# Four modulation products on the four column groups of TensorE, in place of two and two

## The chip, the cores and the metric

One core of one Trainium2 chip runs the whole program in a single launch. The metric is the device time of that launch in microseconds (us); 1860.03 us is the median of the three runs before the change.

## The reference, cut to what matters

The reference computes one layer of a hybrid decoder for a prompt of 1024 tokens and for 8 samples of 8 tokens: gated linear attention beside latent attention, then a feed-forward block with a short convolution. Before all of it stands the modulation, computed from one vector per sequence:

```python
mod = jax.nn.silu(c) @ lw['w_ada'] + lw['b_ada']
sh1, sc1, gt1, sh2, sc2, gt2 = [m[:, None, :] for m in jnp.split(mod, 6, axis=-1)]
h = rmsnorm(x, lw['g_pre_mix']) * (1.0 + sc1) + sh1
z = h @ lw['w_in']
...
x = x + gt1 * rmsnorm(mix, lw['g_post_mix'])
h2 = rmsnorm(x, lw['g_pre_ffn']) * (1.0 + sc2) + sh2
...
x = x + gt2 * rmsnorm(y, lw['g_post_ffn'])
```

There are nine vectors `c` (one for the prompt, eight for the samples) of 1024 values, and `w_ada` is 1024 x 6144 in float32, so each of the six sections of `mod` is the product of a 9 x 1024 matrix with a 1024 x 1024 matrix.

## The kernel before, in words

The kernel is written in Python against a tile framework. The program is traced in program order; a planner then puts the instructions of each engine into an order by a simulation of its own, by priority (which follows program order) and by when it thinks that operands and buffers are ready. A tile taken from a pool waits until one of the pool's buffers of that tag is free; any free buffer serves.

**A section of the modulation** (`ada_section`, line 235) has two halves of 512 columns. For one half, the sum over 1024 rows is cut into eight parts of 128 rows (`k` = 0 to 7). The stationary operand is `cT[:, k]`, 128 x 32 (nine columns used), the moving one a piece of `w_ada` of 128 x 512. Part k goes to the group of 32 columns of TensorE with number k mod 4, so its result lands on partitions 32 (k mod 4) to 32 (k mod 4) + 31 of the tile `adaps`; parts k and k + 4 add up in the same place. A float32 product shows in the trace as two matmul instructions with two weight loads. The four partial sums are added later: by a small product with a selection matrix (`mod_T`, line 292, tile `modps`) for sections 0, 1, 3 and 4, and by VectorE (`ada_gate`, line 261, tiles `gpart` and `M`) for the gate sections 2 and 5. The weights come in tiles `wraw` of 128 x 2 x 512 (512 KB), one for two parts. So a half has four steps, each a load and two products (four matmul instructions on two column groups), and a `yield` behind each.

**Who drives it.** The program's first stage (`phase1`, line 352) runs sections 1 and 0 to their end at once (lines 382 and 388), with 16 buffers of `wraw`. The other four sections (3, 4, 2, 5) belong to the generator `ada` (line 437). It is advanced by one `next(ada, None)` ahead of each group of products of the input projection: nine times in the loop over the key and value columns (line 486, the tile `zps` has 320 columns there), twelve times in the loop over q and k (line 509, 384 or 320 columns), and nine times in each of the two loops over v and r (line 537, 512 columns). The first six of these 39 calls run `gates`; the next 32 are the modulation's steps; the last one finishes. A group of the projection is 24 matmuls (`mm3`, lines 141 to 143: high and low parts of float32 values).

**The buffers.** In this part `wraw` has four buffers, which the steps share with the projection's weights: `load_w` (line 280) loads a `wraw` tile, ScalarE copies it to `whi` (line 288), VectorE or GpSimd makes `wlo` (line 122), and then the buffer is free. `whi` and `wlo` have six buffers each, and a set of weights (`group`, line 398) takes four, so two of the next set's four loads keep their `wraw` buffers until the set in use is done with. All loads and nearly all stores are issued by SyncE (its queue is SP) in the planner's order.

Behind this stage follow the queries, gated linear attention interleaved with the attention over the samples' cached keys (to about 915 us), the output projection and the two halves of the feed-forward block.

Of the kernel before, what the change touches and what calls it, by code (L numbers as in the profile page):

```python
# [11 lines left out]
F32 = mybir.dt.float32  # L12
# [9 lines left out]
P = 128  # L22
D = 1024
# [83 lines left out]
class Kernel:  # L107
# [127 lines left out]
    def ada_section(self, sec, wp, pp, bufs, evac, rp=None):  # L235
        nc, A = self.nc, self.A
        w = A["w_ada"][0].rearrange("(a p) n -> p a n", p=P)
        rb = bufs[0]
        for half in range(2):
            ps = pp.tile([P, 512], F32, name="adaps", tag="A")  # L240
            for k2 in range(4):
                c0 = sec * D + half * 512
                raw = (rp or wp).tile([P, 2, 512], F32, name="wraw", tag="wraw", bufs=rb)
                nc.sync.dma_start(raw, w[:, 2 * k2:2 * k2 + 2, c0:c0 + 512])

                for kk in range(2):
                    k = 2 * k2 + kk
                    r = slice(32 * (k % 4), 32 * (k % 4) + 32)
                    nc.tensor.matmul(ps[r], self.cT[:, k, :], raw[:, kk, :], start=(k < 4), stop=(k > 3))
                yield 0.5  # L250
            evac(ps, half)

# [1526 lines left out]
```

## Time and profile before

| | |
|---|---|
| median of 3 runs (1857.51 to 1861.93) | 1860.03 us |
| the profiled execution's own time | 1861.26 us |
| its span, first to last instruction | 1859.5 us |
| TensorE busy in it | 1797.6 us (97%) |
| mean granted clock of TensorE | 0.985 of full speed |

The three runs lie within 0.24% of each other. The span is the stretch that the profile shows; the execution's own time is 1.76 us longer. The sums below are made against the profiled execution.

### The profile page before, as it was taken

How to read it: one execution, taken by the hardware profiler on the slowest of the kernel's cores; microseconds unless marked ns; L12 is line 12 of the kernel's file. 1: busy time of each engine (PE TensorE's matmuls, PEld its weight loads, DVE VectorE, ACT ScalarE, POOL GpSimd, SP SyncE). 2: the span in 40 equal slices, each digit the busy share in tenths (PEclk: the TensorE clock that was granted, in tenths of full speed). 3: DMA queues.
4: the chain of work that ended last, by engine and by line, in shares of the span. 5: the costliest groups of instructions: out<-in, count | busy, mean ns of one | idle time of the engine just before them, and what ended most of it. 6: DMA issues, size and time to landing. Idle time of an engine off the chain costs nothing.

```text
span 1859.5 us, 30758 instructions
## 1 busy us (share of the span) xinstructions
PE 1797.6 (97%) x12403; PEld 1500.4 (81%) x12403; DVE 930.1 (50%) x1680; ACT 708.9 (38%) x1398; POOL 529.8 (28%) x567
## 2 busy tenths in 40 slices
PE   6999999999999999999799999999999999999998
PEld 3888766765665776777499999999999999788787
DVE  3731233347784555565556755554545554523433
ACT  2461111455666666667523422222222222323322
POOL 2640100423554223323011133333333331202221
PEclk7999999999999999999899999999999999999999
DMA  8255552666655555455542412111222111834463
GB/s 300 87 160 181 181 172 75 248 210 199 212 197 166 203 196 173 161 184 181 181 149 104 137 65 71 65 59 65 72 70 70 65 61 61 266 98 136 146 183 96
DMA packets 170618, 265.26 MB, mean 143 GB/s; under 512 B 18278, under 2 KB 118694, under 8 KB 162283
## 3 DMA queue, kind: packets, MB, share of 16 engines
q1 hardware_dynamic: 156138, 179.39, 29.8%
q0 software_dynamic: 14336, 83.89, 13.0%
q8 instruction: 98, 1.61, 0.4%
q14 instruction: 46, 0.37, 0.1%
HBM read 221.49 MB, written 41.75 MB: 142 GB/s over the span
## 4 chain that ended last, share of the span: by engine, by line
PE 70%; DVE 3%; DMA 2%; ACT 1%; issue 1%; SPq 0%; POOL 0%; DVEq 0%; POOLq 0%; ACTq 0%
PE ups L141 9%; PE ups L143 9%; PE ups L142 9%; PE kps L1227 6%; PE yps L143 4%; PE yps L141 4%; PE yps L142 4%; PE S L1237 3%; PE O L1271 3%; PE y L141 2%; PE y L143 2%; PE y L142 2%; PE S L1239 1%; PE lps L705 1%; PE sps L141 1%; PE sps L142 1%
## 5 line engine op out<-in xcount | busy, mean ns | idle before, releaser
L141 PE MATMUL ups<-gh,uhi 128*128 128x384 f32 (+1 forms) x1056 | 347.2, 329 | 0.3 <-DVE hraw L343 0.3
L142 PE MATMUL ups<-gl,uhi 128*128 128x384 f32 (+1 forms) x1056 | 346.7, 328 | 0.0
L143 PE MATMUL ups<-gh,ulo 128*128 128x384 f32 (+1 forms) x1056 | 346.5, 328 | 0.0
L1565 DVE TENSOR_SCALAR cv<-u,vt 128x1024 f32<-128x1024 f32 (+1 forms) x88 | 133.2, 1535 | 216.3 <-ACT u L1555 179.3
L141 PEld LDWEIGHTS ups<-gh,uhi 128*128 128x128 f32 x1056 | 198.3, 188 | 0.7 <-DVE hraw L343 0.6
L143 PEld LDWEIGHTS ups<-gh,ulo 128*128 128x128 f32 x1056 | 198.3, 188 | 0.1
L142 PEld LDWEIGHTS ups<-gl,uhi 128*128 128x128 f32 x1056 | 198.3, 188 | 0.0
L1229 ACT COPY KT<-kps 128x512 f32<-128x512 f32 x256 | 145.3, 587 | 101.3 <-PE kps L1227 100.3
L122 POOL TENSOR_TENSOR ulo<-uraw,uhi 128x2048 fp32r<-128x2048 f32 x24 | 111.4, 4643 | 207.6 <-ACT uhi L1393 204.7
L1555 ACT COPY u<-ups 128x384 f32<-128x384 f32 (+1 forms) x130 | 57.6, 444 | 278.7 <-PE ups L143 278.7
L1227 PEld LDWEIGHTS kps<-ident,L 128*128 128x128 f32 x1024 | 111.5, 141 | 62.0 <-issue 43.4
L1227 PE MATMUL kps<-ident,L 128*128 128x128 f32 x1024 | 153.3, 280 | 4.1 <-ACT KT L1229 2.5
L143 PE MATMUL yps<-uhi,gl 128*128 128x512 f32 x341 | 133.3, 392 | 5.2 <-DVE gl L122 5.2
L141 PE MATMUL yps<-uhi,gh 128*128 128x512 f32 x341 | 133.2, 391 | 0.0
L142 PE MATMUL yps<-ulo,gh 128*128 128x512 f32 x341 | 133.1, 391 | 0.0
L122 DVE TENSOR_TENSOR gl<-graw,gh 128x1408 fp32r<-128x1408 f32 x31 | 59.1, 1908 | 130.2 <-ACT gh L1612 130.2
L1218 POOL DMA_INDIRECT R<-cache_krope,idx x64 | 66.5, 1039 | 179.3 <-PE kps L1227 141.4
L1612 ACT CAST gh<-graw 128x1408 fp32r<-128x1408 f32 (+1 forms) x35 | 45.7, 1306 | 158.7 <-PE yps L142 130.1
L1393 ACT CAST uhi<-uraw 128x2048 fp32r<-128x2048 f32 (+1 forms) x38 | 70.8, 1862 | 92.5 <-PE ups L142 67.1
L141 PE MATMUL zps<-whi,hh 128*128 128x512 f32 (+2 forms) x256 | 96.0, 375 | 0.0
L143 PE MATMUL zps<-whi,hl 128*128 128x512 f32 (+2 forms) x256 | 94.2, 368 | 0.8 <-DVE hl L122 0.8
L1571 POOL TENSOR_TENSOR gl<-gl,cv 128x1088 f32<-128x1088 f32 x22 | 56.0, 2544 | 135.3 <-ACT gl L1570 135.3
(443 smaller groups left out, 3803.5 us busy)
## 6 DMA issues: line engine op xcount, KB each, us to landing
wraw<-w_ada SPq DMA_DIRECT2D x48, 512.0 KB
uraw<-w_ffn_up SPq DMA_DIRECT2D x22, 1024.0 KB
graw<-s_g SPq DMA_DIRECT2D x32, 704.0 KB
s_g<-gl SPq DMA_DIRECT2D x22, 544.0 KB
uraw<-w_ffn_down SPq DMA_DIRECT2D x10, 1024.0 KB
xt<-x_prompt SPq DMA_DIRECT2D x16, 512.0 KB
wraw<-w_in SPq DMA_DIRECT2D x12, 512.0 KB
uraw<-w_o SPq DMA_DIRECT2D x4, 1024.0 KB
```

Source lines behind the costliest of these rows:

```text
L122: eng.tensor_tensor(out, x, hi.bitcast(F32), ALU.subtract)
L141: mm(out, wh, xh, start=start, stop=False)
L142: mm(out, wh, xl, start=False, stop=False)
L143: mm(out, wl, xh, start=False, stop=stop)
L1218: nc.gpsimd.indirect_dma_start(R.rearrange("p j l -> p (j l)"), None, ck, io)
L1227: nc.tensor.transpose(ps[:, k], x, self.ident)
L1229: nc.scalar.copy(KT[:, q // 2, j0:j0 + 4] if q < 4 else KR[:, 4 * half:4 * half + 4], ps)
L1237: nc.tensor.matmul(S[r], Q[:, c], KT[:, c, :, r], start=(c == 0), stop=False)
L1393: self.nc.scalar.copy(hi, raw)
L1555: copy(u[:, 2 + c0:2 + c0 + m], ps[:, 0:m])
L1565: nc.vector.tensor_scalar(yv[z], sh(2)[z], self.cw2[:, ch:ch + 1], self.cb[:, ch:ch + 1], ALU.mult, ALU.add)
L1571: nc.gpsimd.tensor_tensor(gl, gl, res[0], ALU.mult)
```

## The change

A half of a section takes two loads of `wraw` (four parts) in one step, yields, and in the next step runs the four products on the four column groups, one after the other in program order; then the same for the other four parts. The number of loads, of products and of yields stays. A step now is either two loads or four products (eight matmul instructions).

```diff
         for half in range(2):
             ps = pp.tile([P, 512], F32, name="adaps", tag="A")
-            for k2 in range(4):
-                c0 = sec * D + half * 512
-                raw = (rp or wp).tile([P, 2, 512], F32, name="wraw", tag="wraw", bufs=rb)
-                nc.sync.dma_start(raw, w[:, 2 * k2:2 * k2 + 2, c0:c0 + 512])
-
-                for kk in range(2):
-                    k = 2 * k2 + kk
-                    r = slice(32 * (k % 4), 32 * (k % 4) + 32)
-                    nc.tensor.matmul(ps[r], self.cT[:, k, :], raw[:, kk, :], start=(k < 4), stop=(k > 3))
+            c0 = sec * D + half * 512
+            for k4 in range(2):
+                raws = []
+                for k2 in (2 * k4, 2 * k4 + 1):
+                    raws.append((rp or wp).tile([P, 2, 512], F32, name="wraw", tag="wraw", bufs=rb))
+                    nc.sync.dma_start(raws[-1], w[:, 2 * k2:2 * k2 + 2, c0:c0 + 512])
+                yield 0.5
+
+                for k in range(4):
+                    r = slice(32 * k, 32 * k + 32)
+                    nc.tensor.matmul(ps[r], self.cT[:, 4 * k4 + k, :], raws[k // 2][:, k % 2, :], start=(k4 == 0), stop=(k4 == 1))
                 yield 0.5
             evac(ps, half)
```

## Rows read from the trace of the kernel before

**Rows 1.** The page's head: the span and the number of instructions.
```profile
span 1859.5 us, 30758 instructions
```

**Rows 2.** Busy time by stretch: length, busy us of each engine, granted clock, DMA share, GB/s.
```profile
0.00:35.00 35.00, 21.99 (x114) 8.23 (x114) 8.45 (x23) 5.71 (x10) 2.73 (x11) 0.89 0.87 307
...
124.00:313.00 189.00, 188.65 (x906) 137.27 (x906) 52.39 (x94) 24.23 (x45) 19.00 (x16) 1.00 0.51 162
...
321.00:915.00 594.00, 572.08 (x5457) 400.65 (x5455) 338.83 (x962) 369.71 (x848) 207.33 (x238) 0.99 0.56 190
```

**Rows 3.** Matmuls that read `wraw`, 124 to 313 us: count, ns min/median/max, first and last start.
```profile
L249 PE MATMUL adaps<-wraw,cT x128: 592/605/617, 123.9 to 308.9; 128*32 128x512 f32 x128
```

**Rows 4.** Timeline of TensorE (start, us) around the first step in the projection.
```profile
123.56 0.31 PE L142 MATMUL zps<-wlo,hh 128*128 128x320 f32 x1
123.71 0.30 PE L143 MATMUL zps<-whi,hl 128*128 128x320 f32 x1
123.94 1.05 PE L249 MATMUL adaps<-wraw,cT 128*32 128x512 f32 x4
124.93 0.42 PE L141 MATMUL zps<-whi,hh 128*128 128x320 f32 x1
125.19 0.31 PE L142 MATMUL zps<-wlo,hh 128*128 128x320 f32 x1
```

**Rows 5.** Timeline of TensorE around the fifth step, which follows `modps`.
```profile
143.37 0.34 PE L142 MATMUL zps<-hl,whi 128*128 128x384 f32 x1
143.54 0.34 PE L143 MATMUL zps<-hh,wlo 128*128 128x384 f32 x1
143.72 0.96 PE L297 MATMUL modps<-sel,M 106*128 106x9 f32 x8
144.60 1.05 PE L249 MATMUL adaps<-wraw,cT 128*32 128x512 f32 x4
145.58 0.45 PE L141 MATMUL zps<-hh,whi 128*128 128x384 f32 x1
145.87 0.34 PE L142 MATMUL zps<-hl,whi 128*128 128x384 f32 x1
```

**Rows 6.** Timeline of TensorE: line 1237, four products on four column groups.
```profile
496.48 1.06 PE L1237 MATMUL S<-KT,Qd 128*32 128x512 f32 x8
497.48 0.65 PE L758 MATMUL ops<-v,att 64*64 64x128 f32 x6
...
499.23 1.07 PE L1237 MATMUL S<-KT,Qd 128*32 128x512 f32 x8
500.22 0.66 PE L1227 MATMUL kps<-ident,L 128*128 128x128 f32 x4
```

**Rows 7.** Timeline of the weight loads for the first of these.
```profile
496.48 0.16 PEld L1237 LDWEIGHTS S<-KT,Qd 128*32 128x32 f32 x8 [0.17 <-issue]
```

**Rows 8.** All waits of TensorE from 124 to 321 us (total, times, longest).
```profile
PE adaps L249 <- DMA wraw<-w_ada: 0.4, 1, 0.4
```

**Rows 9.** Timeline of the SP queue: issues of loads.
```profile
129.28 0.39 SPq L244 DMA_DIRECT2D wraw<-w_ada  x1
...
131.32 0.45 SPq L244 DMA_DIRECT2D wraw<-w_ada  x1
...
161.10 0.37 SPq L287 DMA_DIRECT2D wraw<-w_in  x1
```

**Rows 10.** Timeline of ScalarE: copies of the projection's weights.
```profile
135.94 1.05 ACT L288 CAST whi<-wraw 128x1024 fp32r<-128x1024 f32 x1 [1.96 <-PE zps L143]
...
164.75 1.05 ACT L288 CAST whi<-wraw 128x1024 fp32r<-128x1024 f32 x1 [4.14 <-DMA wraw<-w_in]
```

**Rows 11.** Waits of the SP queue, 124 to 313 us: the largest (total, times, longest).
```profile
SPq L244 <- PE adaps L249: 45.7, 17, 6.1
```

**Rows 12.** Timeline of weight loads: last step of the first half of section 1.
```profile
10.44 0.15 PEld L249 LDWEIGHTS adaps<-wraw,cT 128*32 128x32 f32 x4 [1.19 <-DMA wraw<-w_ada]
```

**Rows 13.** Timeline of TensorE where the projection ends.
```profile
320.48 0.40 PE L143 MATMUL zps<-whi,hl 128*128 128x512 f32 x1
320.71 1.04 PE L885 MATMUL qps<-ident,wm 128*128 128x128 f32 x8
```

## The prediction

> **What bounds the kernel now.** I read the busy time by stretch first. The page gives a span of 1859.5 us [rows 1]; the stretches say where TensorE is the bound. From 124 to 313 us, where the projection runs with the modulation's steps between its groups, TensorE is busy 188.65 of 189.00 us at a granted clock of 1.00, while VectorE has 52.39 and the DMA engines are at 0.51 [rows 2]. The list of TensorE's waits says the same from the other side: between 124 and 321 us it waited once for another engine or a transfer, 0.4 us for a load of w_ada [rows 8]. So in this stretch a microsecond less on TensorE is a microsecond less in the end, as long as nothing else comes late. Up to 35 us it is otherwise: the DMA engines are at 0.87 with 307 GB/s, and TensorE is busy 21.99 of 35 us [rows 2]; the weight loads of a half's last step wait 1.19 us for their transfer [rows 12].
>
> Then I counted the steps that the change touches: 128 matmul instructions at four a step are 32 steps, from 123.9 to 308.9 us [rows 3]. All lie in the stretch that TensorE bounds. The other 64 of line 249 belong to sections 1 and 0, before 35 us.
>
> **What one step costs now.** The timeline shows more than the step's 1.05 us. The projection's matmuls of 320 columns start 0.15 us apart (123.56, 123.71). From the last of them to the step it is 0.23 us, from the step to the next matmul 0.99, and from that one to its follower 0.26 [rows 4]. So a step inserts 0.08 in front, 0.99 itself, 0.11 behind: 1.18 us. The loss in front and behind is paid for each change between the two kinds of products.
>
> Four of the steps (the fifth, ninth, 13th and 17th) stand behind `modps`, since the sums of a finished half of sections 3 and 4 are taken there. There the step itself takes 0.98 us, and the matmul after it 0.29 to its follower where 0.17 to 0.18 is usual, 0.11 more [rows 5]. Without the step, `modps` itself would stand before the projection's matmul, and what that change costs no row shows: at least nothing, at most the same 0.11. So such a step gives back 0.98 to 1.09 us; I take 1.04, the middle.
>
> **What four at a time cost.** The trace has this very shape elsewhere. Line 1237 sends four products of a 128 x 32 stationary and a 128 x 512 moving operand, float32, to the four column groups. From its eight instructions to the next matmul it is 1.00 us (496.48 to 497.48) and 0.99 (499.23 to 500.22) [rows 6]. Eight instructions cost what four do now: two column groups leave half the array's columns idle for the same time. So four products take 1.00 us where two took 0.99.
>
> The change's 16 quads stand where the 2nd, 4th, ... 32nd step stands now, since the yields stay as many and the loads take the odd ones; the odd steps' products go. All four steps behind `modps` are odd ones. The sum:
> - 12 odd steps of 1.18 us: 14.2 us less.
> - 4 odd steps behind `modps` of 1.04 us: 4.2 us less.
> - 16 quads, 0.01 us dearer than a step: 0.2 us more.
> Together 18.2 us less.
>
> The Trainium skill has a rule that speaks against this. "TensorE: Matmul & The Clock Gate", section "Part 3: Packing small matmuls — row/col tiling", says that a weight load overlaps with matmuls in flight only if its row group differs; here all four products use all rows, so by the rule the loads of one column group would wait for the products of another. The trace does not agree: the eight loads of such a quad begin within 0.16 us together, while the products run [rows 7]. By the rule, a quad would be two pairs after each other and the sum 2.5 us, worked out as the first rival below; by the rows it is 18.2.
>
> **What else moves.** In the first stage the loads are the same in number and order, and a half ends when its last load lands and that step's products are done; a quad takes 0.01 us more than a pair, so I cost this at nothing. The cover is the transfer; what could go wrong is that TensorE, with its work in fewer bursts, is granted the lower clock for one more quad, about 1 us for each of four halves at most. The copies out of `adaps`, the sums on VectorE and the `modps` products follow the second quad of a half, at the call of `next` that they follow now. VectorE has 137 us free in the stretch [rows 2].
>
> Behind 313 us everything hangs on TensorE's end of the projection: the first work of the queries starts 0.23 us after its last matmul, without a wait [rows 13]; its weights are asked for at line 521, ahead of the v and r loops. So the 18.2 us shift all that follows. The planner works out its order from simulated times, so orders behind this stage can change; that may go either way, and I put no price on it in the sum.
>
> **The loads.** Here the change can give something back. Two of the four `wraw` buffers are held for long by the projection's next weights: their copy waits for TensorE to be done with the set in use (1.96 us at 135.94, behind the projection's matmul) [rows 10]. With two buffers left, a step's load now runs while the other step's products wait. A quad needs both buffers and frees both at its end, so the next pair can be issued only then, and must land within two groups of the projection: 48 matmuls of 0.147 us, 7.1, and 0.2 for the changes, 7.3 us in the kv loop, for the second quad; 48 of 0.175, 8.6 us in all, in the q and k loop, for about three quads [spacings from rows 4, 5]; longer with 512 columns.
>
> A load that ran alone took 3.65 us from issue to its copy (161.10 to 164.75) [rows 9, 10]. The second of a pair is bounded by 512 KB at the 307 GB/s of the first stretch [rows 2], 1.7 us more, and by a full 3.65 more: the pair lands 5.4 to 7.3 us after issue. SP comes to a freed buffer late: the first step's buffer was free at 124.93 and its load issued at 129.28, 4.35 us after; the second's (step at 123.94 + 24 x 0.147 + 1.18 = 128.65, free at 129.64) at 131.32, 1.7 after [rows 4, 9]. From below, 5.4 + 1.7 = 7.1 us: no wait at all. From above, 7.3 + 4.35 = 11.65 us: 4.4 us at the second quad and 3.05 at each of three others, 13.5 us. I take nothing, the lower end: over the stretch SP stood ready before the buffer was free 17 times, 45.7 us in total [rows 11], so the 4.35 is the exception, and of all these loads one made TensorE wait, 0.4 us [rows 8].
>
> **The rivals.**
> 1. The change does not do what it says: the quad runs as two pairs after each other, 2 x 0.99 us, 0.99 more than a step now. Of the 18.4 us of the odd steps, 16 x 0.99 come back, and 2.5 stay, the losses in front and behind. 1861.26 - 2.5 = 1858.8 us, 1857.5 against the median: no change that a measurement can tell. [Rows 6, 7] speak against it. 3%.
> 2. The pairs come late in the stretches with two buffers: 3 to 13.5 us of the 18.2 go, most likely about 6, the kv loop's wait and part of the others. 1844 to 1855 us, about 1848. For it speaks the kv loop, where even the lower sum leaves 0.2 us; against it the planner, which can put a quad some matmuls later into a group without a wait. 15%.
> 3. Slower: the same wait, but at all 16 quads. It decides from a mean wait of (18.2 + 3.7) / 16 = 1.4 us on, that is, when a pair lands 10 us after its buffers come free also where four buffers are free. At the upper 13.5 us for four quads and 1.4 to 3 us at the 12 others it is 30 to 50 us given up out of a gain of 18.2, so 1872 to 1892 us, about 1880. Against it stand the DMA engines at 0.51 and the single wait of 0.4 us [rows 2, 8]. 3%.
> 4. The planner orders the stage from 321 to 915 us otherwise. TensorE is idle 22 us there [rows 2], so a better order can gain a few us, and a worse one lose some 6 (a quarter more idle time): 1836 to 1849 us, either side of the forecast. 7%.
>
> **How the numbers follow.** 1861.26 - 18.2 = 1843.1 us for the profiled execution, whose time is 1.23 us over the median; against the median, 1841.8, so 1842 us. This case holds 72%, and its own range, with the bounds of the four steps behind `modps` (0.2 us), the first stage (up to 4 us) and the spread of the runs, is 1838 to 1846. For 8 in 10 the range reaches into rivals 2 and 4: 1836 to 1850. What a measurement can tell from no change is about 0.2%, 3.7 us. Faster: the forecast, rivals 2 and 4, and none of the others, less a little for a late pair that takes nearly all: 0.93. Same: rival 1 and that remainder, 0.04. Slower: rival 3, 0.03.
>
> **What the changed profile would show.** Line 249 with as many instructions as before (128 from 124 us on), but in 16 bursts of eight that last about 1.06 us, the next matmul 1.00 us after the burst's start. TensorE's end of the projection near 302 us where 320.7 stands now. TensorE's waits from 124 to 302 us at most 1 us; a wait for w_ada at the second quad of 2 to 4 us would be rival 2. Eight weight loads within 0.2 us; loads that come in two clusters per quad would be rival 1. The prediction is wrong if the pairs wait in many places, if the bursts last near 2 us, or if the stages behind 321 us change their length by more than about 3 us.

## The result and the profile after

The changed kernel takes 1846.45 us (median of 6 runs, 1842.06 to 1848.54), the kernel before beside it 1859.94 (6 runs, 1856.79 to 1861.93). The ratio is 0.9923 with a 95% interval of 0.9911 to 0.9935: 0.77% of 1859.94, or 14.3 us less (12.1 to 16.6), where 18.2 were forecast; the two medians lie 13.5 us apart. That is faster, inside the range of 1836 to 1850, and 0.45 us above the upper end of the forecast's own range of 1838 to 1846. The profiled execution took 1848.54 us, 12.7 less than that of before. Two lines are added ahead of the projection, so line 249 is now 251, `modps` 299, the load of `wraw` 246.

First the page's head of the changed kernel, which answers to [rows 1], and its busy time by stretch, with the columns of [rows 2]:

```profile
span 1846.8 us, 30762 instructions
```

```profile
0.00:35.00 35.00, 23.17 (x109) 9.07 (x110) 8.12 (x23) 6.27 (x10) 2.51 (x11) 0.81 0.87 312
124.00:304.24 180.24, 180.24 (x931) 140.60 (x929) 56.73 (x98) 24.22 (x42) 17.24 (x16) 1.00 0.53 172
304.24:896.00 591.76, 574.18 (x5458) 402.04 (x5458) 335.45 (x947) 366.15 (x841) 205.43 (x236) 0.99 0.57 191
```

The projection's stretch is the one that is shorter, and TensorE still bounds it. The lower granted clock up to 35 us (0.81, where it was 0.89) is not the change's: in the second profile of the same kernel, below, it is 0.95, and in the kernel whose first stage is as before it is 0.81 again. A *quad* below is four products in one step, eight matmul instructions, as in the prediction; a *burst* is any such run of products of `adaps` between matmuls of the projection. The timeline of TensorE in the changed kernel (start, length) shows the first quad, the second, `modps` standing alone, the seventh quad, the 13th, and the projection's end:

```profile
126.06 0.31 PE L143 MATMUL zps<-whi,hl 128*128 128x320 f32 x1
126.30 1.06 PE L251 MATMUL adaps<-wraw,cT 128*32 128x512 f32 x8
127.30 0.42 PE L141 MATMUL zps<-whi,hh 128*128 128x320 f32 x1
...
134.30 0.30 PE L143 MATMUL zps<-whi,hl 128*128 128x320 f32 x1
134.53 1.98 PE L251 MATMUL adaps<-wraw,cT 128*32 128x512 f32 x8
136.44 0.44 PE L141 MATMUL zps<-hh,whi 128*128 128x384 f32 x1
...
140.71 0.96 PE L299 MATMUL modps<-sel,M 106*128 106x9 f32 x8
141.52 0.42 PE L141 MATMUL zps<-hh,whi 128*128 128x384 f32 x1
141.78 0.33 PE L142 MATMUL zps<-hl,whi 128*128 128x384 f32 x1
...
183.81 1.39 PE L251 MATMUL adaps<-wraw,cT 128*32 128x512 f32 x8
185.13 0.44 PE L141 MATMUL zps<-hh,whi 128*128 128x384 f32 x1
...
250.83 1.05 PE L251 MATMUL adaps<-wraw,cT 128*32 128x512 f32 x4
251.81 0.50 PE L141 MATMUL zps<-whi,hh 128*128 128x512 f32 x1
...
252.93 1.04 PE L251 MATMUL adaps<-wraw,cT 128*32 128x512 f32 x2
253.91 0.50 PE L151 MATMUL zps<-wlo,h 128*128 128x512 f32 x1
...
255.74 1.05 PE L251 MATMUL adaps<-wraw,cT 128*32 128x512 f32 x2
256.71 0.50 PE L142 MATMUL zps<-wlo,hh 128*128 128x512 f32 x1
...
304.01 0.39 PE L143 MATMUL zps<-whi,hl 128*128 128x512 f32 x1
305.08 0.33 PE L887 MATMUL qps<-ident,wm 128*128 128x128 f32 x1 [0.69 <-ACT vst L545]
```

From the first quad to the next matmul it is 1.00 us (126.30 to 127.30), as line 1237 had it [rows 6]; 13 of the 16 quads take 0.99 to 1.00. Three do not. The second takes 1.91 us, the seventh 1.32. The 13th stands in three bursts of four, two and two instructions, 0.98, 0.98 and 0.97 us, with matmuls of the projection between them: 18 bursts, not 16. The weight loads of these quads (start, length, idle before and its releaser) tell why two are long:

```profile
126.30 0.16 PEld L251 LDWEIGHTS adaps<-wraw,cT 128*32 128x32 f32 x8 [0.19 <-issue]
...
134.53 0.14 PEld L251 LDWEIGHTS adaps<-wraw,cT 128*32 128x32 f32 x4 [0.19 <-issue]
...
135.45 0.14 PEld L251 LDWEIGHTS adaps<-wraw,cT 128*32 128x32 f32 x4 [0.78 <-DMA wraw<-w_ada]
...
184.15 0.14 PEld L251 LDWEIGHTS adaps<-wraw,cT 128*32 128x32 f32 x4 [0.20 <-DMA wraw<-w_ada]
```

The second pair of products waits for the second load of its pair. The SP queue of the changed kernel shows when the two were issued, one group of 0.94 us. It is the next thing that SP does after six stores of `kvst`, one every 0.4 to 0.6 us from 126.61 on; the last of them and the pair:

```profile
129.09 0.40 SPq L499 DMA_DIRECT2D s_kv<-kvst  x1
129.59 0.94 SPq L246 DMA_DIRECT2D wraw<-w_ada  x2
```

The list of SP's waits (total, times, longest), from 124 to 303 us, shows how seldom SP now stood ready ahead of a free buffer, 5 times where it was 17 [rows 11]; part of that is that two loads now wait together:

```profile
SPq L246 <- PE adaps L251: 12.6, 5, 4.9
```

From the first quad to the projection's last matmul it is 177.71 us (126.30 to 304.01). Before, it was 191.83 from the second step (128.65, the prediction's) to 320.48 [rows 13], and 1.18 for the first step, which the change removes: 193.01. So the stretch gives 15.3 us.

### The profile page after: what moved, and what is told of

Its sections match the earlier page's. It is cut to its first block, busy times and chain, and to the rows that moved or that the text cites. A ratio compares the mean times of both kernels' runs of the same rounds, so it can differ in the third digit from the quotient of the medians.

```text
span 1846.8 us, 30762 instructions
## 1 busy us (share of the span) xinstructions
PE 1785.6 (97%) x12403; PEld 1500.2 (81%) x12403; DVE 932.3 (50%) x1680; ACT 709.4 (38%) x1398; POOL 528.4 (29%) x567
## 4 chain that ended last, share of the span: by engine, by line
PE 71%; DVE 4%; DMA 2%; ACT 1%; issue 1%; POOL 0%; SPq 0%; DVEq 0%; POOLq 0%; ACTq 0%
PE ups L141 10%; PE ups L143 10%; PE ups L142 10%; PE kps L1229 6%; PE yps L143 4%; PE yps L141 4%; PE yps L142 4%; PE S L1239 3%; PE O L1273 3%; PE y L141 2%; PE y L142 2%; PE y L143 2%; PE S L1241 1%; PE lps L707 1%; PE sps L141 1%; PE sps L142 1%
## 5 line engine op out<-in xcount | busy, mean ns | idle before, releaser
L1614 ACT CAST gh<-graw 128x1408 fp32r<-128x1408 f32 (+1 forms) x35 | 45.7, 1307 | 160.3 <-PE yps L142 133.1
```

## The experiments

The question was where 4 of the 18.2 us went. Theory A puts them into the stretch itself: four `wraw` buffers are too few for pairs, which shows as the waits at the second and seventh quad and as the torn 13th. Theory B puts them behind the projection, whose stages would run longer than before. The first four kernels ran on one chip, beside 23 runs of the kernel before (1863.37 us, 1858.73 to 1866.88).

**The changed kernel again.** No edit.

> The changed kernel itself, timed again in five rounds so that the variants beside it can be compared with it on one chip. Theory A (the gain is what the projection's stretch gives back: 18.2 us by the sum, less 1.2 us for two quads whose second pair of products waits for its load, less 2.4 us for the 13th quad, which the planner tore into three bursts) expects a ratio to the kernel before of 0.992, about 14.5 us less. Theory B (the projection gave more, and the stages behind it took some back) expects the same ratio; the two are told apart by the runs below.

Measured: 1847.23 us (6 runs, 1842.94 to 1851.21), ratio 0.9917 (0.9898 to 0.9936). Again 18 bursts, the 13th quad torn; the second takes 1.79 us, the seventh 1.00. First quad to last matmul: 177.25 us. From there to the end of the span it is 1538.7 us, where it was 1542.8 in the first profile of the changed kernel and 1539.0 in that of the kernel before. The loss in the stretch repeats (at the second and the 13th quad; the seventh does not wait this time); that behind it does not, which speaks against B.

**Five `wraw` buffers.** Two other tiles give up a buffer to make room.

```diff
-        rb, hb = bufs or (4, 6)
+        rb, hb = bufs or (5, 6)
...
-                    yield from self.ada_mod(sec, slot, wp, pp, (4, 6))
+                    yield from self.ada_mod(sec, slot, wp, pp, (5, 6))
...
-                t = mp.tile([9, 512], F32, name="gpart", tag="gpart", bufs=2)
+                t = mp.tile([9, 512], F32, name="gpart", tag="gpart", bufs=1)
...
-        t1 = xp.tile([P, h, RO], F32, name="rp1", tag=f"rp1{h}", bufs=2)
+        t1 = xp.tile([P, h, RO], F32, name="rp1", tag=f"rp1{h}", bufs=1 if h == 1 else 2)
```

(`ada_gate` and `rp2` likewise.)

> The changed kernel with five wraw buffers in place of four (room is made by one buffer in place of two for gpart and for the rope's small tiles, which VectorE alone writes and reads in the small case). The planner's order then keeps all 16 quads whole. Theory A: the two late pairs and the torn quad go, so the projection ends about 3.6 us earlier than in the changed kernel, and the whole takes about 3.6 us less than it: 1842 to 1843 us where the changed kernel takes 1846. Theory B: the projection ends earlier, but the stages behind it wait for what they waited for before, and the total stays at 1846.

Measured: 1841.46 us (6 runs, 1836.71 to 1845.67), ratio 0.9883 (0.9864 to 0.9902). The timeline of TensorE in this kernel, at the second quad, the 13th and the end of the projection:

```profile
132.60 0.30 PE L143 MATMUL zps<-whi,hl 128*128 128x320 f32 x1
132.83 1.06 PE L251 MATMUL adaps<-wraw,cT 128*32 128x512 f32 x8
133.83 0.44 PE L141 MATMUL zps<-hh,whi 128*128 128x384 f32 x1
...
247.90 1.06 PE L251 MATMUL adaps<-wraw,cT 128*32 128x512 f32 x8
248.89 0.50 PE L141 MATMUL zps<-whi,hh 128*128 128x512 f32 x1
...
298.75 0.40 PE L143 MATMUL zps<-whi,hl 128*128 128x512 f32 x1
```

All 16 quads are whole and take 0.99 to 1.00 us; neither TensorE's matmuls nor its weight loads wait for a transfer of w_ada between 124 and 299 us. What the buffer does for the second quad stands on the SP queue: ahead of the first quad there is now room for three loads of w_ada. In the changed kernel, and in this one:

```profile
97.84 1.85 SPq L246 DMA_DIRECT2D wraw<-w_ada  x2
```

```profile
93.86 4.11 SPq L246 DMA_DIRECT2D wraw<-w_ada  x3
```

By the program's order, one of the second quad's two loads is then long there, and the other is the first of the pair issued at 127.80. SP comes to that pair 2.20 us after the first quad's end, as late as in the changed kernel (2.29). First quad (124.60) to last matmul: 174.15 us, 3.56 and 3.10 less than in the two profiles of the changed kernel. Both the waits and the tear are gone with one buffer more: theory A. (The two small tags that gave up a buffer were not run alone.) The gain over the changed kernel is 5.8 us where 3.6 were expected. The rest of it, between the medians of 1847.23 and 1841.46, is not in the stretch: this kernel's first quad stands 3.3 us ahead of the other's (127.87), which the last section takes up.

**Pairs of loads, products two at a time.** The change's half of the loads, without its half of the products.

```diff
-                yield 0.5
-
-                for k in range(4):
-                    r = slice(32 * k, 32 * k + 32)
-                    nc.tensor.matmul(ps[r], self.cT[:, 4 * k4 + k, :], raws[k // 2][:, k % 2, :], start=(k4 == 0), stop=(k4 == 1))
-                yield 0.5
+                for k2 in range(2):
+                    for k in (2 * k2, 2 * k2 + 1):
+                        r = slice(32 * k, 32 * k + 32)
+                        nc.tensor.matmul(ps[r], self.cT[:, 4 * k4 + k, :], raws[k2][:, k % 2, :], start=(k4 == 0), stop=(k4 == 1))
+                    yield 0.5
```

> One part of the change alone: the loads are asked for two at a time as in the changed kernel, the products still run two at a time, in two steps. Theory A: the loads bring nothing, 32 bursts of 1.18 us stay, the time is that of the kernel before within 2 us (1858 to 1862). A rival, that earlier loads or a different order on the SP queue make a part of the gain, expects 1850 to 1856.

Measured: 1860.27 us (10 runs, 1857.58 to 1865.43), ratio 0.9991 (0.9978 to 1.0003): no change. There are 32 bursts again. On the timeline of TensorE, the first:

```profile
122.94 1.05 PE L250 MATMUL adaps<-wraw,cT 128*32 128x512 f32 x4
123.92 0.42 PE L141 MATMUL zps<-whi,hh 128*128 128x320 f32 x1
```

From the second burst (127.65) to the projection's last matmul (319.22) it is 191.57 us, 0.26 less than before. Loads in pairs alone bring no gain that can be told; it is all in the four products.

**Four products at a time on two column groups.** Parts 0, 1, 4 and 5 go to groups 0, 1, 0, 1 in one step, the others to groups 2 and 3 in the next.

```diff
-            for k4 in range(2):
+            for q in range(2):
                 raws = []
-                for k2 in (2 * k4, 2 * k4 + 1):
+                for k2 in (q, q + 2):
...
-                for k in range(4):
-                    r = slice(32 * k, 32 * k + 32)
-                    nc.tensor.matmul(ps[r], self.cT[:, 4 * k4 + k, :], raws[k // 2][:, k % 2, :], start=(k4 == 0), stop=(k4 == 1))
+                for j in range(2):
+                    for g in (2 * q, 2 * q + 1):
+                        r = slice(32 * g, 32 * g + 32)
+                        nc.tensor.matmul(ps[r], self.cT[:, g + 4 * j, :], raws[j][:, g % 2, :], start=(j == 0), stop=(j == 1))
```

> Four products in one burst as in the changed kernel, from two loads, but on two column groups: parts 0, 1, 4, 5 on groups 0, 1, 0, 1, then parts 2, 3, 6, 7 on groups 2, 3, 2, 3. Only the losses in front of and behind a burst are saved, not the time of the products. Theory A: a burst lasts 1.84 to 1.98 us to the next matmul; with two bursts torn in two by the planner the gain is 3 to 5 us, so 1855 to 1857 us. If the gain came from fewer bursts alone and not from four groups side by side, it would be as fast as the changed kernel, 1846.

Measured: 1859.48 us (10 runs, 1855.25 to 1863.30), ratio 0.9983 (0.9970 to 0.9995). On the timeline of TensorE, a burst of the same eight instructions now takes 1.84 us to the next matmul (130.98 to 132.82):

```profile
130.74 0.31 PE L143 MATMUL zps<-whi,hl 128*128 128x320 f32 x1
130.98 1.91 PE L252 MATMUL adaps<-wraw,cT 128*32 128x512 f32 x8
132.82 0.41 PE L141 MATMUL zps<-whi,hh 128*128 128x320 f32 x1
```

This is the prediction's rival 1, built: as many loads, steps and yields as in the changed kernel, with the products as two pairs one after the other. The weight loads come as the prediction said they would for this rival, in clusters: four begin at 130.97 us, two at 131.43, two at 131.86. All rows are in use in both kernels; what differs is whether a load goes to a column group that is still at work. The kernel gives 4.7 us in the stretch (193.01 less 188.35, from 130.98 to 319.33) and 0.17% in all. Rival 1 said 2.5, with 0.99 for each pair; the measured 1.84 is 0.14 less than twice that, 2.2 us over 16 bursts, and 2.5 + 2.2 is the 4.7. (That the two agree to the tenth is chance: two of the bursts are torn here, which takes some back, and the 193.01 is 0.6 us more than the control with five buffers has.) By the medians it is 3.9 us, by the ratio 3.2, in the 3 to 5 that were expected; the time itself is above the expected 1855 to 1857, as the kernel before is slower on this chip too. So of the 18.2 us some 13.5 (16 times 0.84 is 13.4) hang on four column groups running at once, the smaller part on fewer changes between the two kinds of products.

The other four kernels ran on a second chip, beside 13 runs of the kernel before (1866.80 us, 1861.44 to 1869.61).

**The kernel before with five buffers.** A control: the edits of the five-buffer kernel, on the kernel before.

> The kernel before with five wraw buffers (and the same two small tags at one buffer) and nothing else: the control for the run with five buffers. Theory A (five buffers only spare the changed kernel its late pairs and its torn quad): 32 bursts of 0.98 us stay, the single wait of 0.35 us goes, the time is that of the kernel before within 1 us. A rival (the fifth buffer speeds up the loads of the projection's own weights ahead of the first step, where the five-buffer run was already some 3 us ahead at its first quad) expects 3 us less than before, and then only about 3 of that run's 6 us over the changed kernel belong to whole and punctual quads.

Measured: 1864.80 us (10 runs, 1859.73 to 1868.27), ratio 0.9988 (0.9973 to 1.0003): no change that can be told from none. The interval reaches from 5.0 us less to 0.6 more, so it does not exclude the rival's 3 us either, and the first step stands 3.65 us ahead of the kernel before's (120.29 for 123.94). The second of its 32 steps and the projection's last matmul on the timeline of TensorE:

```profile
124.99 1.05 PE L249 MATMUL adaps<-wraw,cT 128*32 128x512 f32 x4
125.98 0.41 PE L141 MATMUL zps<-whi,hh 128*128 128x320 f32 x1
...
316.22 0.40 PE L143 MATMUL zps<-whi,hl 128*128 128x512 f32 x1
```

From the second step on it is 191.23 us, 0.60 less than with four buffers. The fifth buffer is worth 3.1 to 3.6 us in the stretch with quads, 0.6 without; only this difference is the quads', the earlier start is not.

**The changed kernel with five buffers again**, beside its control. No edit to the one above.

> The changed kernel with five buffers again, beside its control on one chip. Both theories: 16 whole quads of 0.99 to 1.00 us, from the first quad to the projection's last matmul 174.2 us as in the first run, within 0.3; the whole 1839 to 1844 us.

Measured: 1844.98 us (4 runs, 1843.55 to 1845.87), ratio 0.9890 (0.9866 to 0.9914). That is 1 us above the 1839 to 1844 expected, on a chip where the kernel before takes 1866.80. The stretch is 174.15 us to the hundredth (124.74 to 298.89). Against the control: 191.23 + 1.18 - 174.15 = 18.26 us. The forecast's sum was 18.2.

**A whole half in one step.** Five buffers, four loads, then eight products; the yields stay as many.

```diff
-            for k4 in range(2):
...
+            raws = []
+            for k2 in range(4):
+                raws.append((rp or wp).tile([P, 2, 512], F32, name="wraw", tag="wraw", bufs=rb))
+                nc.sync.dma_start(raws[-1], w[:, 2 * k2:2 * k2 + 2, c0:c0 + 512])
+                if k2 == 1:
+                    yield 0.5
+            yield 0.5
+            yield 0.5
+            for k in range(8):
...
```

> Five buffers, and all eight products of a half in one step, from four loads asked for in the two steps before. The planner's order has eight whole places of eight products but two halves torn into six and two. Theory A: a burst of eight is two quads after each other, 1.86 us to the next matmul, and spares one loss in front and behind, 0.19 us, and 0.13 at the end of a quad; over eight halves 2.5 us less than the five-buffer run, less 1.2 for each torn half, and less the waits of bursts whose four loads don't fit into the buffers left: where the projection's next weights hold two of five buffers, the last load is asked for only after a product has freed one, so the burst waits 4 to 5 us in its middle. Expected: no faster than the five-buffer run, 1841 to 1850 us. If the loads came in time everywhere, 1839.

Measured: 1847.11 us (4 runs, 1844.57 to 1848.28), ratio 0.9896 (0.9870 to 0.9921): no faster than quads with the same five buffers (0.9890). A whole burst of 16 instructions takes 1.85 to 1.86 us, but two of the eight halves are torn, into six products and two. On the timeline of TensorE, the rest of one waits for its load, and `modps` behind it for VectorE's sums:

```profile
138.97 1.05 PE L252 MATMUL adaps<-wraw,cT 128*32 128x512 f32 x4 [0.81 <-DMA wraw<-w_ada]
140.82 1.06 PE L300 MATMUL modps<-sel,M 106*128 106x9 f32 x8 [0.79 <-DVE M L260]
```

The waits of 4 to 5 us that were expected in the middle of a burst did not come; the longest wait for a load is this 0.81. The same trade one step further: with longer bursts and the same five buffers, tears and a wait came back.

**The first stage as before.** Sections 1 and 0 in pairs, the other four in quads; four buffers.

```diff
+            if sec < 2:
+                for k2 in range(4):
...
+            else:
+                for k4 in range(2):
...
```

> The changed kernel, but sections 1 and 0 (the first stage) in steps of two products as before; four buffers. Theory: the first stage is bound by its loads, so the time is that of the changed kernel within 1 us, and the planner's order has the same 16 quads with the 13th torn in three. If the longer steps in the first stage cost something (their products wait for two loads), this run is 1 to 2 us faster than the changed kernel.

Measured: 1851.40 us (4 runs, 1849.89 to 1851.95), ratio 0.9920 (0.9896 to 0.9944), as the changed kernel: what quads in the first stage are worth, either way, can't be told from nothing. Its 13th quad is torn too, and its second does not wait; its seventh takes 1.08 us. On the timeline of TensorE:

```profile
135.88 1.07 PE L263 MATMUL adaps<-wraw,cT 128*32 128x512 f32 x8
...
184.24 1.16 PE L263 MATMUL adaps<-wraw,cT 128*32 128x512 f32 x8
...
251.02 1.05 PE L263 MATMUL adaps<-wraw,cT 128*32 128x512 f32 x4
...
253.12 1.05 PE L263 MATMUL adaps<-wraw,cT 128*32 128x512 f32 x2
```

First quad to last matmul is 176.55 us (127.65 to 304.20), 2.40 over the 174.15 of the whole quads; 0.08 of it is the seventh quad's, so the tear costs 2.32. Two bursts more at the 1.18 us that an inserted one costs [rows 4] are 2.36.

That the second quad does not wait here, with four buffers, is worth a look at SP's queue:

```profile
129.45 0.95 SPq L258 DMA_DIRECT2D wraw<-w_ada  x2
```

The pair is issued 0.80 us after the first quad's end (128.65), behind the same six stores, where the changed kernel had 2.29, and needs at most the 6.43 us to the second quad. So the wait at the second quad takes two things together: only two buffers, and an SP that comes late to them.

## Why the prediction came out as it did

**The mechanism and its prices were right.** The sum of 18.2 us appears as 18.26 in the stretch where the quads run whole and unhindered. The odd steps' 1.18 holds, measured a second time as the price of each piece torn off (2.32 for two). The quad costs 1.00 us, read beforehand from another line [rows 6, 7]. The four steps behind `modps` were worth a little more than the 1.04 taken: alone, `modps` takes 0.81 us to the next matmul, and that one 0.26 to its follower where 0.17 to 0.18 is usual, so 0.89 with the loss behind; before, the two took 0.88, 0.98 and 0.11 [rows 5]. That is 1.08, at the upper end of the 0.98 to 1.09. The weight loads start within 0.16 us, so the rule that the prediction cited (the Trainium skill, "TensorE: Matmul & The Clock Gate", section "Part 3: Packing small matmuls — row/col tiling") does not hold for these products.

**The step that failed is "I take nothing" for the loads**, a term that was sized too small. At the second quad the sum from below was 7.1 us against 7.3 at hand. Measured from the profile after: 7.23 us at hand (127.30 to 134.53), 8.15 needed (127.30 to 135.45). SP issued the pair 2.29 us after the next matmul began (129.59), where 1.7 was taken from below and 4.35 from above; from issue to the second pair's weight loads it was 5.86, where 5.4 and 7.3 stood. Each lay nearer to its lower end, as the prediction argued, but neither at it, and the margin was only 0.2. This quad lost 0.91 us (1.91 for 1.00), the seventh 0.33: 1.24. The reason given for the lower end was an average: over the whole stretch SP stood ready before the buffer 17 times [rows 11]. From 124 to 143 us, where the second quad falls, only two of those 17 waits lie, 3.1 of the 45.7 us. There SP is held until 125.13 us by the store of `la`, which waits 4.7 us for GpSimd in both kernels, and then works through the six stores of `kvst`. At the seventh quad SP was quick, 0.47 us, and the transfer slow: the pair was issued at 175.49, right behind two loads of w_in (173.94), and its second weight loads began 8.66 us later, beyond the 7.3 that the prediction took as the upper end. In the second profile the same pair was in time. The two issues on SP:

```profile
173.94 1.45 SPq L289 DMA_DIRECT2D wraw<-w_in  x2
175.49 0.94 SPq L246 DMA_DIRECT2D wraw<-w_ada  x2
```

**What no step had is a torn quad.** The prediction named the planner as a reason against rival 2, since it "can put a quad some matmuls later into a group without a wait". It did, but piece by piece, and each piece pays for its own change between the kinds of products: 2.32 us for the 13th quad, more than both waits. TensorE does not wait for a load there. With the fifth buffer this quad is whole, in both runs, so four buffers are most likely behind it; the two small tags that were cut with it were not tried alone, nor by which estimate the planner tore just the 13th.

The two close the account: 174.15 + 2.32 + 1.24 = 177.71 us, measured 177.71; in the second profile, with 0.79 at the second quad alone, 177.26 and 177.25. So the outcome is the forecast with a part of rival 2: it had the place and the cause (two buffers left, pairs late) right, but the waits alone are 1.24 us, below its 3 to 13.5, and they come to 3.6 only with the tear, which it did not have.

**The other rivals.** Rival 1 falls by the 1.00 us of a quad beside 1.84 when the four products have two column groups. Rival 3 needed late loads at 16 quads; there were two. Rival 4: in the changed kernel the instructions of each engine stand in the same order as before, but for those around the modulation's steps, so the stage from 321 us on was not ordered otherwise.

**What lies around the stretch.** The projection's last matmul came 16.5 us earlier (320.48 to 304.01; the prediction had it near 302): 15.3 from the stretch, 1.2 from a start that was earlier already. In the second profile of the changed kernel the first quad started at 127.87, so that lead is not the change's. Behind it 3.8 us were lost in the first profile (1542.8 for 1539.0), hence 12.7. By the prediction's own sign, stages behind 321 us that change by more than about 3 us, this would count against it; the second profile (1538.7) has nothing of it. In the profiles of the four kernels on the first chip that length was 1534 to 1541 us, on the second 1543 to 1546, with quads and without. So theory B finds no support: the length varies with the run and the chip, and no part of it could be tied to the change, though with one profile of each kernel a microsecond or two can't be excluded. The timed 14.3 us and the 15.3 of the stretch agree within the interval. The handoff was rightly put at nothing: `qps` now waits 0.69 us for ScalarE's `vst`, yet the first matmul of line 141 after the projection starts 2.55 us behind its end, as before (2.56).

## What to carry to other kernels

Two products of 32 columns each took the same time as four on all four column groups, so look for pairs that leave groups idle; and price a burst between other products with what it costs in front and behind, since each burst saved, or torn off, is worth that too. Bigger bursts need their operands all at once: count the buffers that are left while others hold theirs. Look at what the queue that issues the loads has to do at that place, not on the average of the stretch. When the sums leave a few tenths of a microsecond, add a buffer or expect to lose some of the gain. A control that gives the buffer to the old kernel tells whether the gain is the buffer's or the change's.

## What was not expected of the hardware

All kernels with four buffers, the kernel before among them, show a lower granted clock from 80 to 90 us, well ahead of the projection's steps; all with five do not, the control included. The same stretch by busy time (columns as in [rows 2]) in the kernel before:

```profile
80.00:90.00 10.00, 7.02 (x33) 6.25 (x33) 6.23 (x12) 3.21 (x11) 6.15 (x10) 0.83 0.01 2
```

in the changed kernel:

```profile
80.00:90.00 10.00, 7.37 (x36) 6.41 (x35) 5.44 (x10) 3.00 (x10) 6.14 (x10) 0.83 0.01 2
```

in the changed kernel with five buffers:

```profile
80.00:90.00 10.00, 7.56 (x49) 6.87 (x48) 6.91 (x13) 4.11 (x14) 6.25 (x11) 1.00 0.01 2
```

and in the kernel before with five:

```profile
80.00:90.00 10.00, 7.56 (x49) 7.15 (x49) 6.74 (x14) 4.60 (x15) 6.95 (x12) 1.00 0.01 2
```

A granted clock of 0.83 is part of the stretch at 1.2 GHz, not 2.4: 33 and 36 matmuls in 7.0 and 7.4 us of busy time here (28 to 39 in all five kernels with four buffers), against 49 in 7.56. In the kernel before, the projection's matmuls of 400 columns start 0.33 us apart from 85.79 to 88.79 us, and 0.18 apart before and after, which costs some 1.5 us. TensorE waits twice for VectorE's `cqn` just ahead, 2.6 us in all with four buffers and 2.4 with five; but with four the second wait is the longer one (1.18 and 1.47 us, and the clock falls behind it), with five the first (1.73 and 0.71). With five the first step or quad starts 1.6 to 3.7 us earlier, so the clock can be a part of that, not all of it; the rest was not followed up. Which of the edits that came with the fifth buffer does it was not tried; in the control's total it can't be told from no change (ratio 0.9988).
